# A third plan for a mixture of experts: rounds of 3, 2, 2 and 1 experts, light experts as 64-row tiles

## The chip, the cores and the metric

The kernel runs on one core of a Trainium2 chip. The metric is the device time of one execution in microseconds. Three runs of the kernel before took 2373.07, 2381.03 and 2368.77 us; their median is 2373.07 us. The profile is one further execution.

## The reference, cut to what matters

256 tokens of 1024 features pass two blocks. The first block has two layers: a mixer each, then a dense feed-forward part in the first layer and a mixture of experts in the second. A second block of other mixers follows. The change touches only the mixture of experts:

```
logits = xt @ router_w                      # [256, 8]
top_v, top_i = lax.top_k(logits, 2)
top_w = softmax(top_v)
gates = sum(one_hot(top_i, 8) * top_w)
y = 0
for e in range(8):
    y = y + gates[:, e] * ((silu(xt @ w1[e]) * (xt @ w3[e])) @ w2[e])
```

w1 and w3 of an expert are 1024 x 3584, w2 is 3584 x 1024, all in float32. Only tokens with a gate other than zero matter to an expert, so there are 512 pairs of a token and an expert for 8 experts. The reference's router, worked out on its inputs with the default seed 0, sends 134, 122, 80, 51, 48, 37, 28 and 12 tokens to the experts, the fullest first.

## The kernel before, in words

Everything is float32 and every product is made from parts: a matrix is split into a high part (rounded, type fp32r) and the rest, and a product is high x high + high x low + low x high. A scheduler orders the instructions of each engine ahead of time by a cost model of its own, within the emitted dependencies; a branch (`tc.If`) is scheduled as a block by itself.

`route` (L801) finds the gates, sorts the experts by their number of tokens into slots 0 to 7 (fullest first), and writes to `idi` the expert of each slot and, at column 16, which plan fits (L880 to L884). `moe` (L1084) loads that number into a register of every engine (L1221) and branches (L1222). The plan `few` holds if slot 0 has at most 192 tokens, slot 1 at most 128 and slot 6 at most 64; else `many` runs.

A tile is a group of tokens that one expert works on. A full tile has up to 128 tokens, its x in a high and a low part, and needs three matmuls for each k-tile of 128 weight rows: high on high weights, high on low weights, low on high weights. A half tile (`half`, L935) has up to 64 tokens; its high and low parts lie side by side as 128 stationary columns, so it needs two matmuls: both parts on high weights, and the high part alone on low weights. After the up products the two halves of the result must be added, so its gate (L970 to L973) takes four instructions, ACT, DVE, ACT, ACT, where a full tile takes one on ACT (L975). Both then have one multiply on DVE (L980). `turn` (L986) transposes and splits the result: full tiles in L999 to L1002, half tiles in L992 to L995.

Weights come in units of 1 MB (`unit`, L168): SP issues one DMA into one of 4 `raw` buffers, ACT writes the high part `wh` (L165), DVE the low part `wl` (L166), each into one of 4 buffers. DVE's instruction is the last that reads `raw`, and a new DMA into that buffer waits for it. An expert has 42 units: 7 phases f of 4 units up (w1 twice, w3 twice, 4 k-tiles of 512 columns) and 2 units down (w2, 2 k-tiles of 1024 columns). `products` (L945) makes 12 matmuls of 512 columns on a unit for a full tile and 8 for a half tile. All 8 experts stream 336 units whatever their tokens are.

`phases` (L1149) puts experts of a round side by side: up(f) of one expert, then down of the phase before, which belongs to the expert before, then turn(f). With one expert in a round the phase before is its own. The sums of down stay in two PSUM banks per tile until `finish` (L1039) puts them back on their tokens; two experts of the first round add theirs into SBUF instead (`ysum`, L1016 to L1024). There are 8 banks. `place` (L1104) makes one-hots for a group of tiles and allots their x from a ring of 4 buffers of [128, 2048]; a full tile takes a buffer, a half tile half of one. `gather` (L905) fills them by matmuls against the one-hots, during the round before.

Plan `few`, by slots: a first round of slot 0 (a full tile and a half tile), 7 (half) and 6 (half) side by side; then slots 1, 2, 3, 4 and 5, one expert to a round, each a full tile.

Of the kernel before, what the change touches and what calls it, by code (L numbers as in the profile page):

```python
# [75 lines left out]
class Acc:  # L76
    """a PSUM region that n matmuls accumulate in; fresh: the first one clears the bank"""
# [11 lines left out]
def weave(main, fill):  # L89
    """emit main; ("wait", us) in it is covered by that much tensor-engine work of fill, ("until", f) by  # L90
    what it takes to make f() true"""
    for kind, t in main:
        while kind == "until" and not t():
            next(fill)
        while kind == "wait" and t > 0:
            r = next(fill, None)
            if r is None:
                break
            if r[0] == "work":
                t -= r[1]  # L100
# [7 lines left out]
class Gated:  # L108
    """a generator that comes to a halt ahead of job n until ready()"""
# [16 lines left out]
def blend(a, b, every):  # L126
    """a, with a step of b emitted after each `every` us of it"""
# [10 lines left out]
class Model:  # L138
# [29 lines left out]
    def unit(self, src, ks, c0, n, layout=None, scale=None):  # L168
        """rows of the k-tiles ks, columns c0.. of a weight, in two float32r parts [128, k, n]; scale: a factor
        [128, 1] for the rows of each k-tile"""  # L170
# [43 lines left out]
    def run_b(self, specs, x, tiles=(0, 1), tmajor=False, after=None):  # L214
        """token-layout products. specs: (src, ks, c0, n, {t: [(Acc, column slice)]}, layout);
        tmajor: all units for one token tile, then for the other; after[t]() is emitted behind tile t,
        after[t, i]() behind unit i of it"""
# [31 lines left out]
    def pipe(self, jobs):  # L249
        """token-layout products of one job after the other, units loaded ahead across them.  # L250
        jobs: (units, x, begin, end), units = [(src, ks, c0, n, layout, scale)] of n columns in all,
        begin() ahead of the products, end(banks) behind them; yields ("job", index) ahead of each"""
# [21 lines left out]
    def specs_b(self, src, nk, c0, n, tiles=(0, 1), layout=None, order=None, per=None,  # L274
                scale=None):
        """units and banks of out[t] = x[t] @ src[:, c0:c0+n]"""
# [7 lines left out]
    def run_a(self, src, c0, n, parts, x, nk=8, layout=None):  # L284
        """feature-layout product; parts: (bank, rows, column offset in bank, column offset in the unit)"""
# [19 lines left out]
    def feat(self, src, c0, nf, x, out):  # L305
        """nf tiles of 128 features, two to a bank: [128, f%2, tok]"""
# [3 lines left out]
    def to_feat(self, src, t, xh, xl):  # L310
        """src [128 tok, 1024] -> xh/xl[:, k, t*128:...] split transposed"""
# [20 lines left out]
    def bcast_row(self, dst, src):  # L332
        """DRAM vector [n] to all partitions of dst [128, n]"""
# [3 lines left out]
    def warm(self, func, after):  # L337
        """has the scalar engine's table for func loaded ahead of its use, once after [128, n] is there"""
# [6 lines left out]
    def rsqrt(self, v, eps):  # L345
        """v = (v + eps) ** -0.5 for a few columns, without a table of the scalar engine"""
# [33 lines left out]
    def project(self, src, orders, x, post, scale=None, first=None):  # L380
        """out = x @ src [., 1024]; the last three units go tile by tile, post(t, banks) behind each tile.
        orders: lists of k-tiles that make up units; first() is emitted behind the first products, self.early()
        ahead of the last"""
# [76 lines left out]
    def mix1(self, l, xt, tr1):  # L460
        """-> the generator of the output projection, begun. tr1() emits the transposes of the second token tile"""
# [156 lines left out]
    def attn1(self, qT, kT, v, bt, neglam, yth, ytl):  # L618
# [37 lines left out]
        def values(hp):  # L656
            """[token, (t, head of the pair, feature)]"""
# [118 lines left out]
    def ln_out(self, gen, g, b):  # L776
        """drains a projection into a layer norm; -> (transposed x, emitter of its second tile)"""
# [23 lines left out]
    def route(self, xt, rw):  # L801
        """by slot: gates, positions of the tokens (far off where they are not routed), expert, token count"""
# [51 lines left out]
        # slots: the experts by their number of tokens, most first. Of the 512 places, no more than three can  # L854
        # have over 128, and the last none over 64
# [28 lines left out]
        nc.vector.tensor_copy(idi[:, 16:17], fit[:, 2:3])  # L884
# [20 lines left out]
    def gather(self, g, parts, xh, xl):  # L905
        """x^T of the tokens that the one-hots g[t] [128 tok, 256 or 512] pick, in two parts. parts: the
        destination [128, 8, n] of each part for columns of g, as (first column, n, high, low)"""
# [18 lines left out]
    def expert(self, tiles, w, acc):  # L926
        """the phases of acc[tok] += gate[tok] * swiglu of the gathered tiles, put back on their tokens: a list of
        (jobs, then), jobs = [(unit arguments, tensor-engine work on the unit, what follows it)]"""
# [4 lines left out]
        def mms(tile, src, k):  # L933
            """(stationary operand, part of the weights, rows of the product)"""
# [5 lines left out]
        def products(tile, src, ks, u, targets):  # L940
            """targets: (Acc, columns of the unit); ks: k-tiles of src"""
# [121 lines left out]
    def stream(self, jobs, ahead=2):  # L1063
        """emits jobs (unit arguments or None, work on the unit, what follows), units loaded ahead of their work"""
# [19 lines left out]
    def moe(self, xt, rw, w1, w3, w2, g2, b2):  # L1084
# [19 lines left out]
        def place(slots):  # L1104
# [4 lines left out]
            for s, off, half in slots:  # L1109
# [11 lines left out]
                if half:  # L1121
                    if not halves:
                        b = xbuf()
                        halves += [b[:, 0:1024], b[:, 1024:]]
# [766 lines left out]
```

## Time and profile before

| what | value |
|---|---|
| median of 3 runs | 2373.07 us |
| profiled execution, first to last instruction | 2376.3 us |
| PE / DVE / ACT busy in it | 2285.2 / 1770.3 / 1410.7 us |
| instructions | 29764 |
| read from HBM in it | 580.43 MB |
| DMA of `moe_w1`, `moe_w3`, `moe_w2` | 336 of 1024 KB |

The page gives only the span of the profiled execution, no time around it; the span is 3.2 us over the median of the runs and lies between the lowest and the highest of them.

How to read the rows: a row of the windows view gives start and end of a stretch in us, its length, then busy us and (xinstructions) of PE, PEld (weight loads), DVE, ACT and POOL, then TensorE's granted clock as a share of 2.4 GHz, the DMA engines' busy share and GB/s. Limited to one tile, it leaves out engines that do not touch the tile. A row of the lines view gives line, engine, operation, output<-inputs, shapes and count, then busy us and mean ns, then idle us of the engine just before these instructions and what ended it. A row of the timeline gives start, us, engine, line and operation, with the idle time before it in brackets. A matmul's length is modelled to its end, and matmuls overlap, so the pace of PE is read from starts. "us to landing" is the time from a DMA's issue to its arrival.

### The profile page before, as it was taken

Reading aid. Unit: us, or ns where it says so; the run is one execution under the profiler, and the core shown is the slowest. Engines: PE = TensorE matmul, PEld = TensorE weight load, DVE = VectorE, ACT = ScalarE, POOL = GpSimd, SP = SyncE. Lnnn points to the kernel's source line nnn. Section 1 sums busy time; section 2 is a strip of 40 time slices with the busy share of each in tenths; the row PEclk is TensorE's granted clock in tenths of the full one; section 3 lists DMA queues with packets and bytes.
Section 4 is the critical chain, followed back from the end, with each engine's and each line's share of the span. In section 5 each row is a group of like instructions: output and inputs, shape, how many; then the busy total and the mean of one; then the engine's idle time right before and its main releaser. Section 6 shows DMA issues by size and latency. Waiting matters only on the chain. (4 is left out here: it accounts for less than half of the span.)

```text
span 2376.3 us, 29764 instructions
## 1 busy us (share of the span) xinstructions
PE 2285.2 (96%) x11444; PEld 1854.5 (78%) x11444; DVE 1770.3 (74%) x1907; ACT 1410.7 (59%) x1532; POOL 109.3 (5%) x154
## 2 busy tenths in 40 slices
PE   7999999799999989999999998899999999999998
PEld 6788886577777768887888776787888888888887
DVE  4665465798888998889888887898566459966653
ACT  5554354577777767677777775547554344764542
POOL 2100010100000000000000000100100001010000
PEclk9999999899999999999999999899999999999999
DMA  9456560699999989999999998553655554555552
GB/s 289 171 194 181 177 206 22 230 337 342 343 341 315 322 317 350 348 361 353 375 336 368 358 347 302 190 179 116 213 183 182 195 184 131 183 168 199 181 187 75
DMA packets 266967, 585.10 MB, mean 246 GB/s; under 512 B 10513, under 2 KB 21189, under 8 KB 266560
## 3 DMA queue, kind: packets, MB, share of 16 engines
q1 hardware_dynamic: 260880, 565.48, 68.7%
q0 software_dynamic: 5936, 17.64, 2.4%
q8 instruction: 91, 1.49, 0.3%
q14 instruction: 60, 0.49, 0.1%
HBM read 580.43 MB, written 2.64 MB: 245 GB/s over the span
## 5 line engine op out<-in xcount | busy, mean ns | idle before, releaser
L166 DVE TENSOR_TENSOR wl<-raw,wh 128x2048 fp32r<-128x2048 f32 (+2 forms) x532 | 1200.9, 2269 | 391.6 <-ACT wh L165 389.4
L165 ACT ACTIVATE wh<-raw 128x2048 fp32r<-128x2048 f32 (+2 forms) x532 | 1003.5, 1895 | 515.4 <-PE lin L84 145.1
L945 PE MATMUL lin<-wh,ring 128*128 128x512 f32 x1680 | 556.1, 392 | 0.0
L945 PE MATMUL lin<-wl,ring 128*128 128x512 f32 (+1 forms) x1008 | 399.0, 396 | 9.4 <-DVE wl L166 9.3
L945 PEld LDWEIGHTS lin<-wh,ring 128*128 128x128 f32 x1680 | 315.4, 188 | 81.2
L945 PEld LDWEIGHTS lin<-wl,ring 128*128 128x128 f32 (+1 forms) x1008 | 171.3, 170 | 63.2 <-DVE wl L166 23.2
L84 PE MATMUL lin<-wh,hh 128*128 128x512 f32 x352 | 142.0, 404 | 0.0
L84 PE MATMUL lin<-wl,hh 128*128 128x512 f32 x352 | 138.4, 393 | 2.3 <-DVE wl L166 2.3
L84 PE MATMUL lin<-wh,hl 128*128 128x512 f32 x352 | 138.0, 393 | 0.1
L945 PE MATMUL y<-wl,uh 128*128 128x512 f32 x336 | 107.6, 401 | 3.8 <-DVE wl L166 3.8
L1427 DVE SCALAR_TENSOR_TENSOR ro<-conv,ro 128x256 f32<-128x256 f32 x240 | 105.5, 474 | 0.4
L945 PE MATMUL y<-wh,ul 128*128 128x512 f32 x336 | 104.3, 391 | 0.0
L945 PE MATMUL y<-wh,uh 128*128 128x512 f32 x336 | 104.1, 390 | 0.0
L84 PE MATMUL lin<-wh,h2h 128*128 128x512 f32 x256 | 101.1, 395 | 0.0
L84 PE MATMUL lin<-wl,h2h 128*128 128x512 f32 x256 | 99.9, 390 | 0.2
L84 PE MATMUL lin<-wh,h2l 128*128 128x512 f32 x256 | 99.3, 390 | 0.2
L84 PE MATMUL lin<-wh,xah 128*128 128x512 f32 (+1 forms) x240 | 87.7, 366 | 0.7 <-ACT xah L165 0.6
L84 PE MATMUL lin<-wh,xal 128*128 128x512 f32 (+1 forms) x240 | 86.7, 364 | 0.0
L84 PE MATMUL lin<-wl,xah 128*128 128x512 f32 (+1 forms) x240 | 86.6, 361 | 0.0
L84 PEld LDWEIGHTS lin<-wl,hh 128*128 128x128 f32 x352 | 66.8, 190 | 16.1 <-DVE wl L166 3.2
L84 PEld LDWEIGHTS lin<-wh,hh 128*128 128x128 f32 x352 | 66.8, 190 | 15.7 <-issue 1.3
L84 PEld LDWEIGHTS lin<-wh,hl 128*128 128x128 f32 x352 | 66.7, 189 | 14.7 <-DVE hl L166 0.4
(543 smaller groups left out, 3781.0 us busy)
## 6 DMA issues: line engine op xcount, KB each, us to landing
raw<-in_moe_w SPq DMA_DIRECT2D x336, 1024.0 KB, 6.8
raw<-in_w_in SPq DMA_DIRECT2D x70, 1024.0 KB, 5.2
raw<-in_w_ff SPq DMA_DIRECT2D x64, 1024.0 KB, 5.2
raw<-in_ffn_w SPq DMA_DIRECT2D x32, 1024.0 KB, 5.1
raw<-in_w_out SPq DMA_DIRECT2D x12, 1024.0 KB, 8.2
raw<-in_w_branch SPq DMA_DIRECT2D x8, 1024.0 KB, 5.9
raw<-in_w_out SPq DMA_DIRECT2D x8, 512.0 KB, 8.3
raw<-in_w_branch SPq DMA_DIRECT2D x8, 512.0 KB, 6.4
```

Of the source, the lines that this page charges most:

```text
L84: nc.tensor.matmul(o, lhsT=lhsT, rhs=rhs, start=(self.i == 0 and self.fresh), stop=(self.i == self.n - 1), skip_group_check=True)
L165: self.nc.scalar.activation(h, src, AF.Copy)
L166: self.nc.vector.tensor_sub(l, src, h.bitcast(F32))
L945: nc.tensor.matmul(a.ap[:rows], lhsT=lhsT, rhs=u[part][:, kk, cs], start=(a.i == 0), stop=(a.i == a.n - 1), skip_group_check=True)
L1427: nc.vector.scalar_tensor_tensor(acc[:, f], uT[:, f, k:k + 256], cw[:, f, k:k + 1], acc[:, f], op0=OP.mult, op1=OP.add)
```

## The change

A number 2 in column 16 of `idi` stands for a third plan, `light`: it holds if `few` holds and slot 3 has at most 64 tokens. Two short DVE instructions in `route` work it out; the branch of two becomes a branch of three, with `light` first. `light` has the first round of `few`, then slots 1 (full) and 5 (half) side by side, then 2 (full) and 4 (half), then 3 (half) alone. That makes slots 3, 4 and 5 half tiles, which were full ones. The list of left over half buffers now outlives a call of `place`, so that the half left over from the first group serves slot 5, and the one left over from slot 4 serves slot 3. Elsewhere the diff only takes out docstrings and comments.

```
-        nc.vector.tensor_copy(idi[:, 16:17], fit[:, 2:3])
+        nc.vector.tensor_scalar(fit[:, 3:4], cs[:, 3:4], 64.5, fit[:, 2:3], op0=OP.is_lt, op1=OP.mult)
+        nc.vector.tensor_add(fit[:, 4:5], fit[:, 2:3], fit[:, 3:4])
+        nc.vector.tensor_copy(idi[:, 16:17], fit[:, 4:5])
...
+        halves = []
+
         def place(slots):
...
-            tiles, parts, c0, halves = [], [], 0, []
+            tiles, parts, c0 = [], [], 0
...
-                        halves += [b[:, 0:1024], b[:, 1024:]]
+                        halves.extend([b[:, 0:1024], b[:, 1024:]])
...
             placed = {}
-
+            halves.clear()
...
-        few = [([(0, 0, False), (0, self.cap, True), (7, 0, True), (6, 0, True)],
-                [[(0, (0, 1), None), (7, (2,), 0), (6, (3,), 1)]])]
+        first = ([(0, 0, False), (0, self.cap, True), (7, 0, True), (6, 0, True)],
+                 [[(0, (0, 1), None), (7, (2,), 0), (6, (3,), 1)]])
+        light = [first]
+        light += [([(s, 0, False), (h, 0, True)], [[(s, (0,), None), (h, (1,), None)]]) for s, h in ((1, 5), (2, 4))]
+        light += [([(3, 0, True)], [one(3)])]
+        few = [first]
...
-        n = nc.values_load(idi[0:1, 16:17], min_val=0, max_val=1)
-        with tc.If(n > 0) as cmp:
-            run(few)
+        n = nc.values_load(idi[0:1, 16:17], min_val=0, max_val=2)
+        with tc.If(n > 1) as cmp:
+            run(light)
         with cmp.Else():
-            run(many)
+            with tc.If(n > 0) as inner:
+                run(few)
+            with inner.Else():
+                run(many)
```

## Rows read from the trace of the kernel before

**Rows 1.** Windows view: first round, single rounds, 60 us of them, first 10 us.

```profile
447.00:861.00 414.00, 398.08 (x1822) 295.10 (x1821) 367.06 (x286) 306.25 (x256) 0.00 (x0) 1.00 0.94 331
861.00:1460.00 599.00, 592.29 (x2675) 481.34 (x2676) 526.16 (x335) 430.20 (x301) 0.00 (x0) 1.00 0.98 355
1260.00:1320.00 60.00, 59.67 (x268) 48.83 (x268) 51.94 (x29) 44.29 (x29) 0.00 (x0) 1.00 1.02 374
440.00:450.00 10.00, 10.00 (x42) 8.21 (x41) 7.57 (x21) 8.49 (x35) 0.00 (x0) 0.92 1.05 393
```

**Rows 2.** Windows view of the tile raw, same first two stretches: DVE, then ACT.

```profile
447.00:861.00 414.00, 295.43 (x130) 247.51 (x131) 1.00 0.94 331
861.00:1460.00 599.00, 459.14 (x202) 386.01 (x202) 1.00 0.98 355
```

**Rows 3.** Lines view, 861 to 1460 us: ACT's split, PE's waits, full tiles.

```profile
L165 ACT ACTIVATE wh<-raw 128x2048 fp32r<-128x2048 f32 x202 | 386.0, 1919 | 123.1 <-DMA raw<-in_moe_w 112.5 <-PE lin L945 4.6 <-DVE sa L980 2.1
L945 PE MATMUL lin<-wl,ring 128*128 128x512 f32 x544 | 215.4, 396 | 5.5 <-DVE wl L166 5.4
...
L166 DVE TENSOR_TENSOR ul<-uT,uh 128x512 fp32r<-128x512 f32 x34 | 23.2, 683 | 2.6 <-ACT uh L165 2.6
L980 DVE TENSOR_TENSOR sa<-sa,lin 128x512 f32<-128x512 f32 x33 | 22.6, 685 | 12.2 <-PE lin L945 11.9
...
L165 ACT ACTIVATE uh<-uT 128x512 fp32r<-128x512 f32 x34 | 20.3, 596 | 25.7 <-PE uT L999 25.6
L975 ACT ACTIVATE sa<-lin 128x512 f32<-128x512 f32 x34 | 20.2, 593 | 14.8 <-PE lin L945 14.6
```

**Rows 4.** Timeline of PE: start of up(f), its 47th matmul, next start.

```profile
1007.30 0.48 PE L945 MATMUL lin<-wh,ring 128*128 128x512 f32 x1
...
1017.83 0.39 PE L945 MATMUL lin<-wl,ring 128*128 128x512 f32 x1
...
1024.22 0.39 PE L945 MATMUL lin<-wh,ring 128*128 128x512 f32 x1
```

**Rows 5.** Timeline of PE, matmuls of a half tile: the first and the eighth.

```profile
510.04 0.40 PE L945 MATMUL lin<-wl,ring 128*64 128x512 f32 x1
...
511.67 0.39 PE L945 MATMUL lin<-wh,ring 128*128 128x512 f32 x1
```

**Rows 6.** Lines view, 447 to 861 us: what half tiles add on DVE and ACT.

```profile
L971 DVE TENSOR_TENSOR sa<-lin,sa 64x512 f32<-64x512 f32 x21 | 14.3, 682 | 0.7
...
L972 ACT ACTIVATE sa<-sa 64x512 f32<-64x512 f32 x21 | 13.3, 632 | 4.6 <-DVE sa L971 4.2
...
L166 DVE TENSOR_TENSOR uhl<-uT,uhl 128x256 fp32r<-128x256 f32 x21 | 8.7, 417 | 0.1
```

**Rows 7.** Page, part 6: weight DMAs, count, KB, us from issue to landing.

```profile
raw<-in_moe_w SPq DMA_DIRECT2D x336, 1024.0 KB, 6.8
raw<-in_w_in SPq DMA_DIRECT2D x70, 1024.0 KB, 5.2
```

**Rows 8.** Timeline of DVE: an instruction of the plan's condition, and the last unit's split.

```profile
434.68 0.20 DVE L883 TENSOR_SCALAR route<-route 128x1 f32<-128x1 f32 x1
...
1467.75 2.29 DVE L166 TENSOR_TENSOR wl<-raw,wh 128x2048 fp32r<-128x2048 f32 x1 [1.58 <-ACT wh L165]
```

**Rows 9.** Timeline of PE: the first matmuls behind the last unit's split.

```profile
1470.09 0.73 PE L945 MATMUL y<-wl,uh 128*128 128x512 f32 x2 [0.70 <-DVE wl L166]
```

**Rows 10.** Windows view of short stretches in which PE waited, for the granted clock.

```profile
100.00:105.00 5.00, 3.07 (x22) 2.73 (x23) 3.92 (x6) 2.72 (x3) 0.71 (x1) 1.00 0.65 210
...
1480.00:1485.00 5.00, 0.00 (x0) 0.00 (x0) 3.46 (x7) 0.29 (x1) 0.97 (x2) 0.50 0.35 119
1495.00:1500.00 5.00, 5.00 (x14) 3.85 (x13) 5.00 (x6) 4.98 (x4) 0.00 (x0) 0.53 0.90 306
```

**Rows 11.** Timeline of PE at half clock: two matmuls of 512 columns.

```profile
1495.47 0.63 PE L84 MATMUL lin<-wh,hh 128*128 128x512 f32 x1
1495.89 0.63 PE L84 MATMUL lin<-wl,hh 128*128 128x512 f32 x1
```

## The prediction

> **What bounds the kernel now.** I read the windows view first, because the change touches one stage: the experts run from 447 us to a little past 1470 us [rows 9], and that is two stretches with different limits, the first round of three experts and then five rounds of one [rows 1]. The change leaves the first round as it is, so the second stretch decides. There PE is busy 592.29 of 599 us, which is 99%. But the DMA engines are busy 98% too, at 355 GB/s. Two resources seem full, and the question is what is left when one is relieved.
>
> Next I counted units. The tile raw shows 202 splits in those 599 us, 2.965 us for a unit [rows 2]. What would each resource need for a unit, if it alone mattered?
>
> PE: from one up(f) to the next in a full tile's steady state is 16.92 us [rows 4], in which lie 72 matmuls of 512 columns on 6 units and 4 transposes: 2.82 us a unit. Gathers and put-backs between experts raise it, and the 99% of rows 1 says that the whole stretch is 2.93 us a unit of PE work.
>
> DMA: a unit is 1,048,576 bytes. The best 60 us moved 374 GB/s, or 2.80 us a unit, but PE was full then too (59.67 of 60), so this shows only what DMA can do at least. The first 10 us, with all raw buffers free, moved 393 GB/s, 2.67 us a unit [rows 1].
>
> DVE: 526.16 us of work over 202 units, 2.60 us a unit [rows 1, 2].
>
> Last I read who waits in the lines view [rows 3]. PE waits for a split only 5.5 us in the row shown, so it is fed. ACT is idle 112.5 us ahead of splits until a DMA has landed, so transfers are not far ahead either. But ACT and DVE, which work in order, also stand 25.6, 14.6 and 11.9 us for PE's results (uh, silu, the multiply). Such a stop delays the splits behind it, they free raw late, and the next DMA starts late. So PE is the tightest, and DMA pays part of PE's delay back as gaps.
>
> **The change part by part.**
>
> *Three full tiles become half tiles (slots 3, 4, 5).* Each of 3 x 42 units has 8 matmuls where it had 12. Eight half-tile matmuls start 1.63 us apart from first to last, 7 intervals of 0.233 us [rows 5], so a half unit is 1.86 us of PE. A full unit's 12 matmuls are at most 2.82 us. PE loses about 0.9 us on 126 units, some 115 us of work. Very little of that can reach the end, because the units still have to arrive: none of the 336 DMAs goes.
>
> *Pairing.* A full and a half expert side by side need (2.82 + 1.86 + 0.07) / 2 = 2.38 us of PE a unit. The 0.07 is a unit's share of the half tile's turn, taken like a full tile's: 46 matmuls of up take 10.53 us, 0.229 each [rows 4], and 16.92 less 72 x 0.229 over 6 units is 0.07. Slot 3 alone needs 1.93. Both are under 2.67, so PE no longer bounds, by either bound for DMA.
>
> *What half tiles add.* On DVE an addition of 682 ns, and a split of 417 where a full tile has 683 [rows 3, 6]: 0.416 us more for each of 21 phases, 8.7 us over 210 units, 0.04 a unit. DVE then needs 2.65. On ACT four short instructions of about 0.6 us where there was one; ACT has 430.20 of 599 us in use [rows 1], so this is covered as long as no wait sits among them (a rival, below).
>
> *What is late next.* With PE at 2.38 and DVE at 2.65, the DMA engines are next, at 2.80 or, at best, 2.67. The bounds of the new pace are then 2.965 (nothing gained) and 2.67. I take 2.80, the rate kept up over 60 us, and add what coupling costs: PE, the tightest, was used 96% in the first round (398.08 of 414) and 99% in the second stretch [rows 1]. At 98% the pace is 2.80 / 0.98 = 2.86 us. Gain: 202 x (2.965 - 2.857) = 21.8 us.
>
> *The end of the stage.* The last unit of the last expert has 8 matmuls instead of 12 behind DVE's last split, where PE waits for it [rows 8, 9]: 12 x 0.229 less 8 x 0.233, 0.9 us less on the path.
>
> *Route.* Two DVE instructions on one column stand ahead of the branch, each like L883 with 0.20 us [rows 8]: 0.4 us more, on the path, since every engine waits for the branch. The nested branch costs nothing where `light` is taken: one comparison falls through, as before.
>
> *Order and buffers.* The number of tiles, gathers, put-backs and register loads is the same; only one-hots padded to 256 columns add four short DVE memsets, hidden in DVE's spare 12%. SP issues the same 336 DMAs in another order of experts. The half of a ring buffer left by slot 6 is written while slot 6 still reads the other half; if the two were ordered against each other, slot 6's next up would wait for copies that are due two experts earlier, so nothing. Two experts' sums hold four PSUM banks where a single one holds two; the first round already lives with four.
>
> Sum against the profiled span: 2376.3 - 21.8 - 0.9 + 0.4 = 2354.0 us. The median of the runs is 3.2 us under that span, so the forecast is 2351 us.
>
> **The rivals.**
>
> *Transfers are already at their limit.* For it: DMA busy 98%, ACT waiting 112.5 us for landings, and 4 raw buffers that give a unit 4 x 2.965 = 11.9 us, of which 6.8 to landing [rows 7], ACT's 1.92 and DVE's 2.29 [rows 3, 8] make 11.0 us; at 2.86 us only 0.4 us would be left for all waits, unless landing gets shorter. It is 5.2 us for the weights of other stages [rows 7]. Against it: 374 GB/s over 60 us. If the mean stays between today's 355 and 360, the gain is 3 to 11 us; at 358, about the middle, the pace is 2.93, the gain 202 x 0.035 + 0.5 = 7.6, and the time 2365 us. The Trainium skill (DMA: Bandwidth & Descriptors, Specifications) gives about 358 GB/s as HBM's limit for a core; by that rule this rival would be the forecast. The trace disagrees: 374 and 393 are above it [rows 1].
>
> *Half tiles slow the other engines (slower).* The place is the gate of a half tile: ACT copies, DVE adds, ACT goes on; ACT stands until DVE has worked through a split of 2.29 us, and splits queue behind. The first round, in which three of four tiles are halves, needs 414 / 130 = 3.18 us a unit [rows 2] with no engine full. At that pace the 168 units of the two paired rounds cost 168 x 0.22 = 36 us more, slot 3 alone gains 42 x 0.11 = 4.6, and the time is 2404 us. It decides from a pace of 3.07 in these rounds. Against it: PE had 398.08 / 130 = 3.06 us of work a unit there, and ACT's wait for the addition was 4.2 us in all 21 cases [rows 6].
>
> *PE gets so idle that its clock falls.* With 1.9 to 2.4 us of work in 2.86, PE waits at every unit. At half clock a matmul takes 0.42 us [rows 11], a pair of experts 10 x 0.42 + 0.14 with its turns, 4.35 us a unit, and slot 3 3.5; 168 x 1.4 + 42 x 0.5 is some 255 us more: 2630 us. The Trainium skill (TensorE: Matmul & The Clock Gate, HAM oscillation) tells of a kernel in which waits for DMA between short bursts let the clock fall at every tile. The rows speak against it: at 100 us PE worked 3.07 of 5 us at a clock of 1.00, and 0.50 is seen where PE did nothing in 5 us [rows 10].
>
> *The plan isn't taken.* The counts of the default inputs (slot 3 has 51 tokens) meet the condition; with other inputs `few` would run as before, with 0.4 us and a longer branch: 2374 us.
>
> **How the numbers follow.** Forecast 0.63, transfers at their limit 0.20, plan not taken 0.04, slow half tiles 0.10, clock 0.03. A measurement of this kernel can tell about 0.5%, 12 us, from no change. Faster by more is the forecast: 0.63. Within it are the transfer limit and the untaken plan: 0.24. Slower: 0.13. The range runs from 2327 (a pace of 2.74, most of the way to the 2.67 of DMA's best and DVE's 2.65) to 2373 (nothing gained); outside are the slow cases and a little at the lower end.
>
> **What would show it.** Right: 42 half-tile gates where there were 21, PE below 90% busy behind the first round, PE's waits for DVE's splits some 110 us, 365 GB/s or more there, 2.86 us a unit, the first round at 414 us as before. The second rival shows as ACT's L972 waiting long for L971, and GB/s below 355 in the paired rounds; the third as a clock below 1.00. The forecast is wrong if the rate stays at 355 with PE idle: then the four raw buffers, not PE, set the pace.

## The result and the profile after

Five runs of the changed kernel took 2382.3 to 2394.17 us, median 2391.9 us; five of the kernel before on the same chip have a median of 2377.15 us. The ratio is 1.0065 [1.0041, 1.0088]: slower by 15 us, where 22 us less had been forecast, and outside the range. The profiled execution (span 2380.5 us, 2382.3 us in all) is the lowest of the five, so its rows show the slowdown at its smallest. The medians below are of all runs; e5 and e8 have one run each far above the others (4382.82 and 2564.2 us), which their ratios leave out.

The windows view of the changed kernel, same two stretches as in [rows 1], and two of 20 us:

```profile
447.00:861.00 414.00, 399.49 (x1834) 296.60 (x1833) 370.05 (x292) 307.46 (x253) 0.00 (x0) 1.00 0.94 331
861.00:1460.00 599.00, 513.97 (x2234) 370.14 (x2232) 522.29 (x351) 440.12 (x333) 0.00 (x0) 0.98 0.98 349
...
1260.00:1280.00 20.00, 17.81 (x86) 13.99 (x85) 15.83 (x15) 13.83 (x13) 0.00 (x0) 0.91 0.97 348
1340.00:1360.00 20.00, 17.70 (x73) 12.20 (x73) 19.20 (x15) 16.22 (x13) 0.00 (x0) 0.91 0.92 322
```

The first round is as it was. Behind it PE has 78 us less to do (513.97 instead of 592.29), and yet fewer units come through: the tile raw shows 199 splits (202 in [rows 2]).

```profile
447.00:861.00 414.00, 296.54 (x131) 248.57 (x131) 1.00 0.94 331
861.00:1460.00 599.00, 451.27 (x199) 376.08 (x199) 0.98 0.98 349
```

That is 3.010 us a unit where 2.965 was and 2.857 was forecast. PE is relieved, DVE is no busier (522.29 instead of 526.16 us), ACT little more (440.12 instead of 430.20), and the rate fell to 349 GB/s. No engine is full, so somebody stands in another's way. The lines view of the same stretch (columns as in [rows 3], which these lines answer to) says who:

```profile
L165 ACT ACTIVATE wh<-raw 128x2048 fp32r<-128x2048 f32 x199 | 378.0, 1912 | 68.4 <-DMA raw<-in_moe_w 55.1 <-PE lin L947 8.1 <-DVE ul L166 1.2
...
L947 PE MATMUL lin<-wl,ring 128*64 128x512 f32 (+1 forms) x531 | 214.9, 405 | 60.4 <-DVE wl L166 59.8
...
L974 ACT ACTIVATE sa<-sa 64x512 f32<-64x512 f32 x20 | 12.6, 630 | 2.2 <-DVE sa L973 1.8
L972 ACT ACTIVATE sa<-lin 64x512 f32<-64x512 f32 x21 | 12.4, 592 | 27.5 <-PE lin L947 27.5
...
L165 ACT ACTIVATE uh<-uT 128x512 fp32r<-128x512 f32 x14 | 8.3, 593 | 6.8 <-PE uT L1001 6.8
L977 ACT ACTIVATE sa<-lin 128x512 f32<-128x512 f32 x13 | 7.8, 596 | 12.8 <-PE lin L947 12.8
L165 ACT ACTIVATE uhl<-uT 128x256 fp32r<-128x256 f32 x20 | 7.7, 385 | 31.6 <-PE uT L994 31.5
```

ACT's wait for transfers was halved (112.5 to 55.1 us), so data now lies there waiting for ACT. What grew is ACT's wait for PE at the gates (L972, L977) and the turns (uhl, uh): 27.5 + 12.8 + 31.5 + 6.8 = 78.6 us, where the kernel before had 25.6 + 14.6. And PE in its turn waits for the splits that ACT did not begin. PE is not late because it is full; it is late because it was fed late. One such stop in the timeline, first ACT:

```profile
1181.81 1.91 ACT L165 ACTIVATE wh<-raw 128x2048 fp32r<-128x2048 f32 x1 [0.27 <-DMA raw<-in_moe_w]
1184.65 1.91 ACT L165 ACTIVATE wh<-raw 128x2048 fp32r<-128x2048 f32 x1 [0.93 <-DMA raw<-in_moe_w]
1188.11 0.59 ACT L972 ACTIVATE sa<-lin 64x512 f32<-64x512 f32 x1 [1.54 <-PE lin L947]
1188.73 1.92 ACT L165 ACTIVATE wh<-raw 128x2048 fp32r<-128x2048 f32 x1
```

then DVE and PE on the unit that ACT split at 1181.81:

```profile
1183.90 2.28 DVE L166 TENSOR_TENSOR wl<-raw,wh 128x2048 fp32r<-128x2048 f32 x1
```

```profile
1186.24 0.45 PE L947 MATMUL lin<-wl,ring 128*64 128x512 f32 x1 [0.72 <-DVE wl L166]
...
1187.68 0.39 PE L947 MATMUL lin<-wl,ring 128*64 128x512 f32 x1
```

The gate needs the product of the unit that was split at 1181.81. That product takes 6.30 us from the start of its split: ACT 1.91, DVE to 1186.18, PE's last 7 of 8 matmuls, which had to wait for the low part, from 1186.24 to 1188.1. On ACT only one further split stands between. At a pace of 2.95 us that split ends 2.95 + 1.92 = 4.87 us after the first one's start, so ACT stands 6.30 - 4.87 = 1.43 us (1.54 here). With two splits between, ACT would get to the gate after 7.82 us and would find the product done.

The order is the scheduler's, fixed before the run. The table counts, in the order of ACT's instructions behind the first round, the splits that stand between the split of the last unit that a gate or a turn needs and the gate or turn itself. A gate needs the second unit of w1. A turn needs the second unit of w3, but in most cases its transposes stand in PE's order among the matmuls of the second down unit (w2), and so the count for turns starts there:

| kernel | gates of half tiles | turns of half tiles | gates of full tiles | turns of full tiles |
|---|---|---|---|---|
| before | none | none | 2 (3 in 4 of 35) | 1 in 24 of 35 |
| after | 1 in 16 of 21 | 1 in 17 of 21 | 2 or 3 | 1 in 9 of 14 |

The half tiles' turns stand where most turns of the kernel before stood; the new thing is the gate at one split. In the first round, with several tiles to a unit, half tiles' gates stand 2 to 4 splits behind in both kernels; that is where [rows 6] were read.

### The profile page after: what moved, and what is told of

Same layout as the page of the kernel before. It is cut to its first block, busy times and chain, and to the rows that moved or that the text cites. A ratio compares the mean times of both kernels' runs of the same rounds, so it can differ in the third digit from the quotient of the medians.

```text
span 2380.5 us, 28986 instructions
## 1 busy us (share of the span) xinstructions
PE 2208.4 (93%) x11024; PEld 1744.8 (73%) x11024; DVE 1777.4 (75%) x1940; ACT 1430.5 (60%) x1574; POOL 107.2 (5%) x154
## 5 line engine op out<-in xcount | busy, mean ns | idle before, releaser
L947 PE MATMUL lin<-wh,ring 128*128 128x512 f32 x1344 | 479.9, 395 | 1.8 <-ACT wh L165 1.6
L947 PE MATMUL lin<-wl,ring 128*64 128x512 f32 (+1 forms) x1008 | 403.4, 400 | 66.3 <-DVE wl L166 65.8
L947 PEld LDWEIGHTS lin<-wh,ring 128*128 128x128 f32 x1344 | 253.6, 189 | 86.4 <-ACT wh L165 6.1
L947 PEld LDWEIGHTS lin<-wl,ring 128*64 128x64 f32 (+1 forms) x1008 | 154.1, 153 | 136.9 <-DVE wl L166 97.9
L947 PE MATMUL y<-wl,uhl 128*64 128x512 f32 x336 | 107.3, 401 | 13.5 <-DVE wl L166 13.4
L947 PE MATMUL y<-wh,uhl 128*128 128x512 f32 x336 | 104.5, 392 | 1.6 <-DVE uhl L166 1.1
L947 PEld LDWEIGHTS y<-wh,uhl 128*128 128x128 f32 x336 | 63.2, 189 | 24.6 <-DVE uhl L166 1.6
L84 PEld LDWEIGHTS lin<-wh,hl 128*128 128x128 f32 x352 | 66.5, 189 | 14.6 <-DVE hl L166 0.4
```

The source lines that it names most:

```text
L84: nc.tensor.matmul(o, lhsT=lhsT, rhs=rhs, start=(self.i == 0 and self.fresh), stop=(self.i == self.n - 1), skip_group_check=True)
L947: nc.tensor.matmul(a.ap[:rows], lhsT=lhsT, rhs=u[part][:, kk, cs], start=(a.i == 0), stop=(a.i == a.n - 1), skip_group_check=True)
```

## The experiments

Three theories at the start. **T1**: engines that work in order stop for PE's products and free the raw buffers late. **T2**: the transfers are at their limit. **T3**: PE waits, its clock falls, and late matmuls delay the rest. A fourth was formed on the way (**T4**: the loop of the four raw buffers). Every group shared its runs of the kernel before, with medians of 2374.8 to 2377.25 us.

### More buffers, pairing without halves, halves without pairing, longer half tiles

**e1**: five raw buffers, paid for with one of the low part's.

```
-        l = self.ph.tile([128, 2048], F32R, tag="wl", name="wl")
+        l = self.pl.tile([128, 2048], F32R, tag="wl", name="wl")
...
-        self.pw = ctx.enter_context(tc.tile_pool(name="pw", bufs=4))
+        self.pw = ctx.enter_context(tc.tile_pool(name="pw", bufs=5))
...
+        self.pl = ctx.enter_context(tc.tile_pool(name="pl", bufs=3))
```

> The changed kernel with five raw buffers instead of four, paid for with three wl buffers instead of four. Theory 1 (four raw buffers, freed late because ACT and DVE stand in order for PE's results, set the pace): a fifth buffer takes up the stops, the pace behind the first round falls from 3.01 us a unit to 2.90 or less, and the time is at least 25 us under the changed kernel's 2392, some 2365 us or less. Theory 2 (transfers are at the limit of what memory gives, about 350 to 358 GB/s): within 8 us of 2392, and the time from issue to landing grows by about a unit's 3 us. Theory 3 (PE's clock falls because PE waits, and late matmuls delay the rest): within 8 us of 2392, clock below 1.00 as before.

Measured: 2416.86 us, ratio 1.0176 [1.0151, 1.0202]. All three expectations missed. The loss lies outside the stretch in question: the weights begin to stream 8.7 us later than in the profiled run of the change, the first round is 4 us longer and what follows the last unit 19 us. In the stretch, a window of 570 us of the tile raw (columns as in [rows 2]) has the same 189 to 190 splits as the changed kernel, first e1, then after:

```profile
870.00:1440.00 570.00, 428.56 (x190) 350.87 (x189) 0.99 0.98 350
```

```profile
870.00:1440.00 570.00, 431.23 (x190) 358.94 (x189) 0.99 0.97 348
```

ACT's lines in e1, 861 to 1460 us, tell why a buffer more did nothing:

```profile
L165 ACT ACTIVATE wh<-raw 128x2048 fp32r<-128x2048 f32 x198 | 368.6, 1907 | 10.9 <-PE lin L948 7.1 <-PE y L948 2.0 <-DMA raw<-in_moe_w 1.4
...
L973 ACT ACTIVATE sa<-lin 64x512 f32<-64x512 f32 x20 | 11.9, 593 | 42.6 <-PE lin L948 42.6
...
L165 ACT ACTIVATE uhl<-uT 128x256 fp32r<-128x256 f32 x19 | 7.3, 386 | 45.4 <-PE uT L995 45.4
```

ACT hardly waits for data (1.4 us) and stands that much longer for PE. The transfers do not limit here; ACT's stops do. The raw buffers were not their cause, and the missing low-part buffer isn't either: in this stretch DVE's subtractions wait 0.4 us for PE.

**e2** pairs full tiles (1 alone, 2 with 3, 4 with 5); as its last round has two experts, the put-back of the last one but one is left out. **e3** keeps one expert to a round, with slots 3, 4 and 5 as half tiles.

```
e2: -        light += [([(s, 0, False), (h, 0, True)], [[(s, (0,), None), (h, (1,), None)]]) for s, h in ((1, 5), (2, 4))]
e2: -        light += [([(3, 0, True)], [one(3)])]
e2: +        light += [([(1, 0, False)], [one(1)])]
e2: +        light += [([(s, 0, False), (s + 1, 0, False)], [[(s, (0,), None), (s + 1, (1,), None)]]) for s in (2, 4)]
e3: +        light += [([(1, 0, False)], [one(1)])]
e3: +        light += [([(2, 0, False), (3, 0, True)], [one(2), one(3, 1)])]
e3: +        light += [([(4, 0, True), (5, 0, True)], [one(4), one(5, 1)])]
```

> Pairing alone: slot 1 alone, then slots 2 and 3, then 4 and 5 side by side, all as full tiles, so PE's work is that of the kernel before. Theory 1: PE is as busy as before, and between a product and what waits for it lies the other expert's work, so ACT's waits for PE get shorter: 2365 to 2378 us. Theory 2: as before, 2372 to 2380. Theory 3: clock 1.00, as before, 2372 to 2380. Over 2385 would mean that pairing itself costs, by its PSUM banks or its order.

> Half tiles alone: slots 3, 4 and 5 as half tiles but one expert to a round, as in the plan before. PE's work is that of the changed kernel. Theory 1: with nothing between a product and what waits for it but its own next units, ACT and DVE wait longer for PE than in the changed kernel: 2390 to 2410 us. Theory 2: 2372 to 2390, as transfers do not care. Theory 3: half tiles alone leave PE idle for a third of each unit, the mean clock behind the first round is below the changed kernel's 0.98, and the time is above 2392.

Measured: e2 2380.02 us, 1.0007 [0.9992, 1.0023]; e3 2387.14 us, 1.0048 [1.003, 1.0065]. Pairing costs nothing; the half tiles cost.

**e4** gives half tiles of the later rounds a third matmul for each k-tile, a repeat of the low product (counted twice), so that a unit has 12 again.

```
-                return ((src[:, k, :], 0, 128), (src[:, k, 0:64], 1, 64))
+                pad = ((src[:, k, 0:64], 1, 64),) if len(tiles) == 1 and tile.get("sum") is None else ()
+                return ((src[:, k, :], 0, 128), (src[:, k, 0:64], 1, 64), *pad)
```

> The changed kernel, but half tiles of the rounds behind the first make three matmuls for each k-tile again: the one on low weights is made twice, so the product by low weights is counted twice in them. PE's work is that of the kernel before. Theory 1: PE's results come no earlier, ACT's waits are as long or longer: 2388 to 2410 us. Theory 2: 2380 to 2395, nothing changes for the transfers. Theory 3: PE no longer waits, its clock is back at 1.00 in all of the stage and the time goes back to 2372 to 2380.

Measured: 2383.94 us, 1.0037 [1.0023, 1.005]. Half as many matmuls again on half tiles, and 8 us less than the change. The edit touched the order: half tiles' gates now stand two splits behind in 19 of 21. That the scheduler, counting shorter products, had put them closer is read from this one edit, not shown otherwise. T1, as it stood, had expected other times in all four runs (e2 by 2 us only): a buffer more gained nothing, and more work on PE made nothing slower. What is left of it is ACT's order, which is tested next.

### The order of ACT's instructions

**e5** is the change plus one rule: behind the first round a gate or turn is scheduled only after ACT's split of the last unit loaded by then.

```
-            self.split(h[:, :m], l[:, :m], raw[:, :m])
+            self.last = self.split(h[:, :m], l[:, :m], raw[:, :m])
...
+    def behind(self, tiles):
+        if len(tiles) > 1 or tiles[0].get("sum") is not None:
+            return nullcontext()
+        return self.tc.issue_after(getattr(self.last, "ins", self.last))
...
+                with self.behind(tiles):
+                    gates()
```

> The changed kernel with one rule for the scheduler: on ACT, the gate and the turn's split of a one-tile expert stand behind the split of the unit that was loaded last when they were emitted. In the instruction order that puts two splits, not one, between a unit's own split and the half tile's gate (21 of 21 instead of 5 of 21) and ahead of the turn's split (34 of 34 instead of 9 of 34). Theory 1 (ACT stands in its order for PE's results, one split too early, and everything behind it starts late): ACT's waits for PE behind the first round fall from some 88 us to under 45, and the time falls by 10 us or more, to 2382 or less. Theory 2 (transfers or their four buffers set the pace whatever ACT does): within 5 us of 2392. Theory 3 (PE's idle time and its clock): PE is as idle as before, within 5 us of 2392, clock 0.98.

Measured: 2376.1 us, 0.9994 [0.9983, 1.0005]. The whole slowdown is gone, some 16 us, with the same work on every engine. Its gates and turns stand two or three splits behind (DVE's subtraction of a turn moved along, by one split in most cases), and ACT's lines (861 to 1460 us) answer to those of after:

```profile
L165 ACT ACTIVATE wh<-raw 128x2048 fp32r<-128x2048 f32 x202 | 385.8, 1915 | 115.6 <-DMA raw<-in_moe_w 102.4 <-DVE wl L166 3.7 <-PE y L948 3.3
...
L977 ACT ACTIVATE sa<-lin 64x512 f32<-64x512 f32 x21 | 12.5, 595 | 2.1 <-PE lin L948 1.6
...
L165 ACT ACTIVATE uhl<-uT 128x256 fp32r<-128x256 f32 x20 | 7.7, 384 | 3.6 <-PE uT L1003 3.2
```

27.5 became 1.6 and 31.5 became 3.2; ACT waits for transfers instead, 102.4 us. T3 falls with it: PE is nearly as idle as in the change (523.39 of 599 us busy, 513.97 there) and the granted clock is 0.98 in both, but the time is back.

**e6** puts gates three splits behind. **e7** takes the gates' need for PE away (they read x, so the result leaves out the first product). **e8** puts e5's rule into the kernel before.

```
e6: +            return [(*job("a", w1, 0, 0), none), (*job("a", w1, 1, 0), none),
e6: +                    (*job("b", w3, 0, 0), gate), (*job("b", w3, 1, 0), mul)]
e7: +                    if n == 1 and z.get("sum") is None:
e7: +                        p = (z["x"] if z["half"] else z["x"][0])[:, 0:4].bitcast(F32).rearrange("p k c -> p (k c)")
```

> As the kernel with the rule, and the gate of one-tile experts is emitted one unit later still, so three splits stand between a unit's split and its gate. Theory 1: waits at the gate go to under 10 us, time 5 us or more under the kernel with two splits, 2375 or less. Theory 2 and 3: within 5 us of 2392.

> The changed kernel, but the gates of one-tile experts behind the first round read their x instead of the first product, so ACT and DVE wait for no product there (the output is another function); the turn and the second product still wait. Theory 1: 40 us of ACT's waits for PE go, some of it reaches the pace: 2382 or less. Theory 2 and 3: 2387 to 2395.

> The same rule in the kernel before, where it only moves the split of the turn (24 of 35 stood behind one split, now all behind two). PE is full there. Theory 1: ACT's 26 us of waiting for the turn go, but PE sets the pace: 2370 to 2378. Theory 2: no change, 2374 to 2380.

Measured: e6 2375.78 us, 0.9996 [0.9979, 1.0012]; e7 2380.02 us, 1.001 [0.9998, 1.0021]; e8 2385.2 us, 1.0033 [1.0021, 1.0045]. e6: once ACT no longer stops, more distance gives nothing (T1 had expected 5 us). e7: with the gates free, but the turns still one split behind in 17 of 21, 12 of the 16 us are back. The turns' stops shrink with them, at the same distance; 861 to 1440 us, where the change has 29.8:

```profile
L165 ACT ACTIVATE uhl<-uT 128x256 fp32r<-128x256 f32 x19 | 7.3, 383 | 12.6 <-PE uT L996 12.5
```

So most of the turns' waiting is passed on from the gates. e8 was a miss: the rule made the kernel before 8 us slower. Its profiled execution is the lowest of its runs and shows no stop that would explain it. That stays open here; e17 bears on it.

So T1, as a matter of order, holds for the slowdown. It does not explain why e5, with PE busy 87%, takes no less than the kernel before.

### What holds e5 at 2.94 us a unit

e5 has 194 splits in the window of 570 us. T2 says the transfers' rate. **e9** reads w1 and w3 in rows of 4 KB instead of 2 KB, e5's instructions in e5's order on PE, ACT and DVE; **e10** and **e11** do the same to after and before.

```
...
-                return (wt, ks, f * 512, 512), work
+                return (wt, [2 * q, 2 * q + 1], min(f * 512, 2560), 1024), work
```

> e5_behind with the MoE's w1 and w3 units read as 2 x 1024 columns instead of 4 x 512: the same megabyte a unit, the same instructions in the same order on PE, ACT and DVE, but rows of 4 KB instead of 2 KB (the weights are then others, so the output is not the reference's). In e5_behind the 16 DMA engines are busy 0.98 of 861:1460 and ACT waits 102 us for transfers; a packet of 2 KB takes 92.6 ns there (354 GB/s over 16 engines), one of 4 KB (w2) 172.9 ns (379 GB/s). T2 (transfers hold the pace once ACT no longer stops): a unit falls from 2.94 us to about 1.049 MB / 379 GB/s / 0.98 = 2.82 us, 202 units times 0.12 = 24 us: 2352 (2345 to 2362). If the loop of the four raw buffers, DVE or the clock holds the pace: 2376, within 4.

> The changed kernel with the same longer rows and its own order of instructions. T1 (ACT and DVE stand in order for PE's products): most of the 15 us stays, as the stops do not depend on the transfer: 2380 to 2392, and above e9_behind_rows4k by over 12. T2 alone: as much lower as e9 is below e5, so 2368 (2361 to 2378).

> The kernel before with the same longer rows. If PE alone set its pace behind the first round, as the prediction read it (2.965 us a unit, PE 99% busy): unchanged, 2374 to 2380. If transfers held the pace there too, beside PE: 2 to 24 us lower.

Measured: e9 2384.21 us, 1.0036 [1.002, 1.0053]; e10 2393.17 us, 1.007 [1.0047, 1.0092]; e11 2378.93 us, 1.0023 [1.0008, 1.0037]. No gain anywhere; e9, 8 us above e5, missed both expectations, and e10 lies 9 us above e9 where T1 had said over 12. e9's profiled execution is its slowest (2392.88 us), so its rows overstate the loss; e11, at 352 GB/s where the kernel before has 354, shows no gain either. The tile raw in e9, then in e5:

```profile
870.00:1440.00 570.00, 428.56 (x189) 358.07 (x189) 0.98 0.96 346
```

```profile
870.00:1440.00 570.00, 440.19 (x194) 368.39 (x194) 0.99 0.99 355
```

What rose is the landing, 7.3 us where e5 has 7.0 (DMA issues, 861 to 1460 us; e9, then e5):

```profile
raw<-in_moe_w SPq DMA_DIRECT2D x197, 1024.0 KB, 7.3
```

```profile
raw<-in_moe_w SPq DMA_DIRECT2D x201, 1024.0 KB, 7.0
```

**T4.** A raw buffer is taken from the issue of its transfer to the end of DVE's subtraction: in e5 7.0 + 1.92 + 2.29 = 11.21 us. Four buffers at 570 / 194 = 2.938 us a unit give each 11.75 us. The 0.54 us between is handing over and short waits. In e9 the sum is 11.51 and four times 570 / 189 is 12.06: 0.55 us. That such a sum comes out shows little by itself, since in every kernel here the next transfer is issued 0.03 us after DVE has freed its buffer; what tells is how little of it is waiting. In the change it is 1.2 us (landing 6.6), in e1 with five buffers 4.0 (landing 6.8). So T4 says of e5 and e9: nearly all of a buffer's time is work on its unit, and the four buffers hold the pace. Any time less in the loop should show, any rate of the transfers that does not shorten the landing should not.

**e12**: e5 with e1's five raw buffers.

> e5_behind with the five raw and three low-part buffers of e1. From the 140th to the 330th MoE split e5_behind takes 559.0 us, 2.942 a unit; the whole time is about 33 us longer outside the MoE, as in e1. T2 (the transfers' rate): 559 within 5, the landing grows from 7.0 to about 8.5 to 9.5 us, as one more transfer stands in the queue. The loop of four raw buffers as the bound: 545 or less at a landing of 7 to 7.5.

Measured: 2382.0 us, 1.0031 [1.0019, 1.0044], and in the stretch what T4 gives. The tile raw and the landing:

```profile
870.00:1440.00 570.00, 449.80 (x201) 374.35 (x199) 0.99 1.00 367
```

```profile
raw<-in_moe_w SPq DMA_DIRECT2D x204, 1024.0 KB, 7.5
```

200 units (2.85 us) at 367 GB/s; the 190 units of the expectation took 541.4 us. The window puts the four cases side by side, as splits in 570 us (mean of DVE's and ACT's count):

| | four raw buffers | five raw buffers |
|---|---|---|
| order of the change | 189.5 | 189.5 (e1) |
| e5's order | 194 | 200 (e12) |

The fifth buffer is worth nothing while ACT stops, and 6 units once it does not. (The kernel before has 193: e5 is back at its pace, not beyond.) In e12 the whole time does not gain: its weights begin to stream 8 us later (444.1 instead of 436.0 us), its first round is 5 us longer, and what follows the last unit 14 us. These parts also have one low-part buffer less; that this is the reason was not tested.

**e13** and **e14** shorten the loop without taking a buffer: e5, and behind the first round a unit is split in two halves (e13), which also come as two transfers (e14).

```
-            self.split(h[:, :m], l[:, :m], raw[:, :m])
+            for i in range(0, m, 1024 if halve else m):
+                s = slice(i, min(m, i + (1024 if halve else m)))
+                self.last = self.split(h[:, s], l[:, s], raw[:, s])
e14: -                while j < nk and ks[j] == ks[j - 1] + 1:
e14: +                while j < nk and ks[j] == ks[j - 1] + 1 and not (halve and j * n == 1024):
```

> e5_behind, and behind the first round each weight unit is split in two halves of 1024 columns on ACT and DVE (one transfer a unit, as before), so that DVE subtracts the first half while ACT copies the second. T4 (the loop of the four raw buffers holds the pace once the order is cured: landing 7.0, ACT 1.92, DVE 2.29 and some 0.6 of handing over make 11.8 us, a fourth of it 2.94): ACT's copy of a half is about 1.03 us and DVE's 1.22, worked out from the 512 and 2048 column rows, so a unit holds its buffer 1.03 + 2 x 1.22 = 3.47 instead of 4.21 us; 0.74 / 4 = 0.18 us a unit less, were DVE not then at 2.80 us a unit: 2.85, 190 units in 541 instead of 559 us, and the time 2358 (2352 to 2368). T2 (the transfers' rate): 559 and 2376, within 4.

> The same, and each unit behind the first round comes in two transfers of half a megabyte, so that ACT can begin on the first half while the second is on its way. T4: the buffer is held 1.95 us less behind the landing of its second half (1.03 + 1.22 instead of 4.21), so the loop leaves the pace to DVE (2.80) and to the transfers (2.85 at the 364 GB/s of e12): 2.85 to 2.87, the time 2356 to 2364, or no better than e13. T2: 2376, within 4; more issues on SP (two of 0.37 us a unit) should not show, as SP waits for buffers most of the time.

Measured: e13 2366.0 us, 0.9957 [0.9934, 0.9979]; e14 2360.25 us, 0.9929 [0.9904, 0.9953]. e14 beats both kernels, by 15 us the one before and by 32 us the change. It has 198 units in the window, 2.875 us each; DVE is now the one that hardly waits (the tile raw in e13, then in e14, and e14's lines, 870 to 1440 us):

```profile
870.00:1440.00 570.00, 460.59 (x394) 393.18 (x392) 1.00 0.99 361
```

```profile
870.00:1440.00 570.00, 462.56 (x397) 406.57 (x396) 0.99 0.99 364
```

```profile
L166 DVE TENSOR_TENSOR wl<-raw,wh 128x1024 fp32r<-128x1024 f32 x397 | 462.9, 1219 | 12.7 <-ACT wh L165 11.3
L165 ACT ACTIVATE wh<-raw 128x1024 fp32r<-128x1024 f32 x396 | 406.6, 1056 | 52.7 <-DMA raw<-in_moe_w 46.0 <-DVE wl L166 1.8 <-PE y L951 1.1
```

e13 came out 8 us over what was expected though in its range: four times its pace, 570 / 196.5, fell by 0.15 us, not by the 0.74 that the halves save by themselves. Part of it went to the landing (7.1 us where e5 has 7.0); the rest is waits, which were not taken apart.

### Is the gain the loop's alone, or the half tiles'?

e14's halves in the changed kernel with its own order (**e15**), in the kernel before with its own order (**e16**), and there with e5's rule (**e17**).

> The halved splits and transfers of e14 in the changed kernel with its own order (most gates and turns of the later rounds stand one split behind the unit that they need). T1 and T4 together: with ACT stopped at each gate the shorter loop is worth little, as the fifth buffer was in e1 (570.0 against 570.4 us for 190 units): 2384 to 2392. If the loop alone had been the cause: 2360 to 2368, as e14.

> The halved splits and transfers in the kernel before, its rounds unchanged: two full tiles a round, three products a tile. If PE sets its pace (99% busy): 2373 to 2380, no gain, and the 15 us of e14 are then the worth of the half tiles once their two obstacles are gone. If the loop of four raw buffers held it as well: 2358 to 2368.

> e16 with the gates and turns moved behind as in e8, so that its order is that of e14. PE as the bound: 2373 to 2381. If e8's 8 us were the loop's: lower than e8's 2385 by 5 or more.

Measured: e15 2386.88 us, 1.0052 [1.0032, 1.0072]; e16 2384.23 us, 1.0035 [1.0022, 1.0048]; e17 2372.21 us, 0.9978 [0.9968, 0.9988]. e15: halves without the order are worth 5 us, with it 16. This is no clean pair, as the halves moved e15's order too: 16 of 21 gates of half tiles stand only one half split behind. e16 is the surprise, slower than before by 8 us. Its order had moved too: 29 of 35 gates stand only one unit (two half splits) behind, where e17 has two, and 25 of 35 turns stand ahead of the last half split of the down units. ACT's lines there (861 to 1440 us):

```profile
L165 ACT ACTIVATE wh<-raw 128x1024 fp32r<-128x1024 f32 x385 | 376.7, 1051 | 13.8 <-DMA raw<-in_moe_w 11.5 <-PE lin L948 1.2 <-DVE sa L983 0.4
...
L165 ACT ACTIVATE uh<-uT 128x512 fp32r<-128x512 f32 x33 | 19.8, 599 | 77.4 <-PE uT L1002 77.4
L978 ACT ACTIVATE sa<-lin 128x512 f32<-128x512 f32 x32 | 19.2, 598 | 62.3 <-PE lin L948 62.3
```

62.3 / 32 = 1.9 and 77.4 / 33 = 2.3 us a stop. So the same illness can be given to the kernel before, which had none of the change. e17, with its order mended, has PE full again, in the windows view:

```profile
861.00:1460.00 599.00, 591.66 (x2692) 486.36 (x2690) 537.47 (x540) 463.61 (x508) 0.00 (x0) 1.00 0.97 356
```

e17 lies 13 us below e8, the sign that its expectation named for the loop of the buffers as the source of e8's loss, and 1 us below the range for PE alone. PE is busy 99% there, and 92% in e14. Between e17 and e14, which differ in the plan alone, lie 12.0 us: that is what the half tiles and pairs are worth once neither the order nor the loop stands in the way.

## Why the prediction was wrong

Right: that `light` is taken, with 42 half-tile gates; the first round unchanged; PE below 90% busy; PE as a limit of the kernel before (e17: with loop and order mended PE is still full, at 2372 us, 4 us less). The pace forecast, 2.857 us a unit, was nearly reached by e14 (2.875), but only with two further changes that the prediction did not have. e14's 2360.25 stands 9 us above the forecast: 202 x 0.018 = 3.6 us are the pace, some 3 us that the kernel before itself took 2375 to 2377 us in all later runs where 2373.07 was the base, and the rest is not accounted for. Not as forecast: 349 GB/s instead of 365 or more, and PE's waits for the low part of the weights 76.5 us (59.8 at the row shown) instead of 110.

**The step that failed first** is "What half tiles add": "this is covered as long as no wait sits among them". And, under "What bounds the kernel now", ACT's stops for PE were put down to PE being the tightest, so that a lighter PE would have removed them. The runs show in its place that these stops come from the place of an instruction in ACT's order. With one split between, a gate stops for 1.4 us by the chain of three engines worked out above, 1.6 on average over 16 gates, though PE itself waits in that chain (0.72 us for the low part). The turns then stop as well, mostly for the delay that the gates pass on (e7). The 25.6 and 14.6 us of [rows 3] were the warning: 68 waits of 0.6 us each, now 68 of 1.16. The prediction took the order as given by the kernel before; the change makes a new block, and that is scheduled anew. This alone cost the 15 us (e5 takes them back, and no more).

**The second step** is "I take 2.80, the rate kept up over 60 us", with the transfers as next in line. Next in line was the loop of the four raw buffers. The prediction had its sum (11.0 us against 11.9) and left 0.4 us for all waits at 2.86, but with the page's landing for all 336 units, 6.8 us [rows 7]. In the stretch that matters the kernel before has 7.1 (DMA issues, 861 to 1460 us):

```profile
raw<-in_moe_w SPq DMA_DIRECT2D x201, 1024.0 KB, 7.1
```

With it and the 0.54 us of e5 the loop is 11.85 us, 2.96 a unit, an estimate that is already the pace of before. A lighter PE could gain nothing while that loop stood, as e5 showed. The last sentence on what would show it ("then the four raw buffers, not PE, set the pace") named it; in the rivals it stood only as an argument for the transfers' limit, without a price of its own.

**The rivals.** "Transfers are already at their limit": no. e12 moved 367 GB/s over 570 us and e14 364, where the change moved 348 and e5 355. The Trainium skill (DMA: Bandwidth & Descriptors, Specifications) gives about 358 GB/s for a core; the rate on this core, with nothing else known of its neighbour, was above it over a whole stretch, so that limit did not bind here.

"Half tiles slow the other engines" had the sign at 0.10 and the gate as the place, but not the mechanism: the wait named, ACT for DVE's addition, is 1.8 us in all (L974), and the cost sits at the gate's first instruction and, passed on, at the turns, whose waits the price did not hold. Its sign came out by another cause.

"PE gets so idle that its clock falls": the granted clock is 0.98 in the stretch, with 0.91 in single windows of 20 us. Such a window is a mean of both levels: from 1264.0 to 1267.5 us 0.52 is granted, nearly all of it the lower level (1.2 GHz), after PE had been busy 16.28 of 20 us, while a window with PE busy 15.18 of 20 kept 1.00. e14 has such windows too and is the fastest. At 0.98 a unit's 2.4 us of PE are still under the pace, so it set nothing. The Trainium skill (TensorE: Matmul & The Clock Gate, HAM oscillation) tells of a kernel whose clock falls at every tile for waits on DMA; here PE waited at nearly every unit and no window of 20 us from 860 to 1460 fell below 0.91.

## What to carry to other kernels

Relieving the fullest engine pays only as far as the next closed loop, here the ring of raw buffers: add up, for the stretch itself, how long each buffer is held without waits (landing, copy, subtraction), divide by their number, and compare with the pace before counting on a rate that was seen elsewhere; here 11.21 of 11.75 us left little. On an engine that works in order, count how many units of other work stand between an instruction and the producer of its input; if that many paces are shorter than the producer's chain, the engine stops at each of them, and a change of tile shape can move the count. Two such limits hide one another: the fifth buffer alone gave nothing, the order alone gave back only what was lost, the two together the gain in that stretch.

## What the runs showed of the hardware

Longer rows did not make these transfers faster. In e5's packet records, 870 to 1455 us, a packet of 2 KB takes a median of 84 ns and one of 4 KB 159, which for 16 engines is 390 and 412 GB/s; the means, 92.5 and 173.0 ns, are higher for a few long ones. With all units in 4 KB rows (e9, its slowest run) the mean rose to 180.9 ns, the landing to 7.3 us, and the stretch fell to 346 GB/s. DMA's busy share is 0.96 to 1.00 from 870 to 1440 us in all these kernels at rates from 344 to 367 GB/s: it does not tell whether the transfers are the limit.

Halving an instruction costs little: ACT's copy of 1024 columns takes 1056 ns (e14) where 2048 take 1915 (e5), so two halves take a tenth longer; DVE's subtraction takes 1219 where 2289, 7% longer for two.
